# Mixers and branches with PE in program order, 32-column work gathered with one ada step at a time, denser background queues

## The chip, the cores and the metric

The kernel runs on one core of one Trainium2 chip. The metric is the device time of one execution in microseconds, as the median of several runs. TensorE is called PE, VectorE DVE, ScalarE ACT, GpSimd POOL and SyncE SP.

## What is computed

One layer of a hybrid decoder trunk, in float32, for a prompt of 256 tokens and for 8 samples that each take one step from a stored state. D_MODEL is 2048, a branch is 1024 wide.

```python
mod = jax.nn.silu(c) @ p['w_ada'][l] + p['b_ada'][l]          # six parts: shift, scale, gate, twice
sh1, sc1, gt1, sh2, sc2, gt2 = jnp.split(mod[:, None, :], 6, axis=-1)
h = rmsnorm(x, p['g_pre_mix'][l]) * (1.0 + sc1) + sh1
z = h @ p['w_in'][l]
(z_uv, hq, hf, hi, hg, gq, gk, gv, gr, glr, z_gate) = jnp.split(z, offsets, axis=-1)
...
y_a = spatial_gating(u, v, sgu_w_s, sgu_b_s)                  # A: causal 128x128 mixing per group
o_hg, S_hg = gated_linear_recurrence(q_hg, k_hg, hi, log_f, s_hg[l])   # B: HGRN2, 8 heads of 128 x 128
o_g, S_g = gated_linear_recurrence(q_g, k_g, gv, log_a, s_gla[l])      # C: GLA, 4 heads of 128 x 256
...
merged = gates[:, :, 0] * (branches[0] @ p['w_branch'][l, 0])
for n_b in range(1, N_BRANCH):
    merged = merged + gates[:, :, n_b] * (branches[n_b] @ p['w_branch'][l, n_b])
out = merged @ p['w_out'][l]
x = x + gt1 * rmsnorm(out, p['g_post_mix'][l])
h2 = rmsnorm(x, p['g_pre_mlp'][l]) * (1.0 + sc2) + sh2
y2 = jnp.square(jax.nn.relu(h2 @ p['w_mlp_up'][l])) @ p['w_mlp_down'][l]
x = x + gt2 * rmsnorm(y2, p['g_post_mlp'][l])
```

The recurrence is S_t = diag(f_t) S_{t-1} + k_t v_t^T with o_t = S_t^T q_t for each head; the kernel computes the prompt's by halving (differences over 1, 2, 4, ..., 128 positions), the samples' in one step. Outputs are y for prompt and samples, the final states, and the samples' normalised v rows.

## The kernel before

Activations lie feature by token: 128 features on the partitions, 264 columns (256 prompt tokens and 8 samples). Each weight matrix streams through once in blocks of 512 KB (class `Stream`): a block is loaded by SP three blocks ahead into one of six `raw` buffers and split two blocks ahead into a rounded part `whi` (L102, on ACT) and a remainder `wlo` (L99, on DVE). `granule` multiplies one block with the activations, split likewise: three products for each 128x128 tile (L459, L460, L461), 24 products for a block. A granule is the unit in which the text counts the program's progress. All granules of the program hold 13,872 products.

Other work is written as generators in three queues, which `linear` advances after each granule by the rates in `RATES` (background, samples, ada; another triple in each stage): `bg` holds the mixers, `bs` the samples' steps, `ba` the modulation. A generator runs up to its next `yield`, and the yield's number is what the step cost of the allowance.

- `ada_round` (L247): one part of the modulation. A step (L265) is four products of 32 output columns each, side by side in four strips of the PE array, over 512 streamed columns.
- `mixer_a` (L563): branch A. `mixer_r` (L813): the prompt's recurrence for a group of four heads, two HGRN2 groups and one GLA group. `small_level` (L852) computes a level of the halving in 32 products of 32 x 32; the levels of 32 (L908) and 64 (L916) positions use 32- and 64-column tiles. Then come the keys' transposes (L942), the final states (L950, L951), the outputs (L973 to L976) and their transposes (L995).
- `samples_r` (L762): the samples. Each of 32 steps takes one tile of states `st` (four HGRN2 heads or two GLA heads of one sample), loads the state two steps ahead (L777, three buffers), scales it on ACT (L791), adds the outer product on DVE (L793), stores it from POOL (L794), and reads it on PE with 32-column products (L799).
- `branch` (L1034): eight pairs of a gate product (`zin`) and a branch product with `w_branch`. `parts()`, which finishes the mixer and splits its output for the branch product, is called after the first gate product. `finish` (L1001) transposes the samples' outputs (L1008).

The framework's scheduler places the instructions on every engine, PE too; each engine then works off its list in order. PSUM tiles `sm` for all of the small work have three buffers, the products' accumulators `mm` two.

Of the kernel before, what the change touches and what calls it, by code (L numbers as in the profile page):

```python
# [35 lines left out]
RATES = ((1.7, 0.2, 0.3), (1.5, 0.35, 0.32), (1.5, 0.25, 0.28), (1.0, 0.05, 0.22))  # L36
ST_BUFS = 3
# [9 lines left out]
FILL = (5.0, 9.0)  # L47


@with_exitstack  # L50
def hybrid_step_kernel(
# [53 lines left out]
    # ---------------------------------------------------------------- constants  # L105
# [7 lines left out]
    # ---------------------------------------------------------------- small vectors  # L113
# [7 lines left out]
    # x: prompt rows as two token tiles, the samples' feature tiles as rows  # L121
# [53 lines left out]
    def sum_features(v, n, w):  # L175
        """Sums of v [P, n, w], which it overwrites, over its features (partitions and n tiles), on every partition."""
        while n > 1:
            n //= 2
            add(v[:, 0:n, :], v[:, 0:n, :], v[:, n:2 * n, :])
        ps = sm([P, w])  # L180
        T.matmul(ps, ones, v[:, 0, :], start=True, stop=True)
        return ps

    # ---------------------------------------------------------------- x normed and transposed
    def norm_rows(x, xs, xsn, r):
        """r [P, 2] = the prompt rows' 1 / rms; xsn = the samples' rows xs [P, KT, NS] over their rms."""
# [7 lines left out]
        ps = sum_features(sq, KT, NS)  # L194
# [5 lines left out]
    def transposed(x, k):  # L200
        """Columns of feature tiles k and k + 1 of the prompt rows, in PSUM [P, 2, NP]."""
# [29 lines left out]
    # ---------------------------------------------------------------- adaLN  # L231
# [6 lines left out]
    def ada_rows(acc, n):  # L238
        """PSUM rows (32 j + c, columns) -> [P, i, j, c] with the columns' features on the partitions."""
        am = tmp([P, 512], "am", 1)  # L240
        S.copy(am[:, 0:n], acc[:, 0:n])
        ps = sm()
# [4 lines left out]
    def ada_round(r, pre=()):  # L247
        """Part r of the modulation; pre are its first blocks of weights."""
# [12 lines left out]
        for k in range(KT):  # L261
            if k + 1 < KT:
                ws.append(load(2 * k + 2))
            for j in range(4):
                T.matmul(acc[32 * j:32 * j + 32, :], cT[:, k, :], ws[j // 2][:, j % 2 * 512:j % 2 * 512 + 512], start=k == 0, stop=k == KT - 1)  # L265
            del ws[0:2]
            if k + 1 < KT:
                ws.append(load(2 * k + 3))
# [1027 lines left out]
```

## Time and profile before

| | us |
|---|---|
| median of 3 runs (2008.63 to 2014.89) | 2010.1 |
| span of the profiled execution | 2009.9 |
| PE busy (matmul) | 1948.6, 97% |
| DVE busy | 1191.6, 59% |
| ACT busy | 1002.0, 50% |
| HBM read and written | 439.3 MB, 219 GB/s |

The span lies within 0.2 us of the median, so the profiled execution stands for the timed ones. Products are pipelined: the page's mean of 288 ns is the time from start to end of one product, while the next one starts after less than half of that. So the starts in a timeline tell how fast PE goes, not the durations. The page's chain of waits is on PE for 91% of the span.

### The profile page before, as it was taken

Reading aid. Unit: us, or ns where it says so; the run is one execution under the profiler, and the core shown is the slowest. Engines: PE = TensorE matmul, PEld = TensorE weight load, DVE = VectorE, ACT = ScalarE, POOL = GpSimd, SP = SyncE. Lnnn points to the kernel's source line nnn. Section 1 sums busy time; section 2 is a strip of 40 time slices with the busy share of each in tenths; the row PEclk is TensorE's granted clock in tenths of the full one; section 3 lists DMA queues with packets and bytes.
Section 4 is the critical chain, followed back from the end, with each engine's and each line's share of the span. In section 5 each row is a group of like instructions: output and inputs, shape, how many; then the busy total and the mean of one; then the engine's idle time right before and its main releaser. Section 6 shows DMA issues by size and latency. Waiting matters only on the chain.

```text
span 2009.9 us, 42161 instructions
## 1 busy us (share of the span) xinstructions
PE 1948.6 (97%) x17020; PEld 1814.9 (90%) x17020; DVE 1191.6 (59%) x2105; ACT 1002.0 (50%) x1773; POOL 40.5 (2%) x66
## 2 busy tenths in 40 slices
PE   5999999999999999899899999999999999999997
PEld 4779898989988987789899995999999999999996
DVE  3456566777475687445555556555555555555656
ACT  4434354576664574454444445555444445454543
POOL 1000000000000000000000000000000000000000
PEclk9999999999999999999999999999999999999998
DMA  9887978787798668887555866655555555555552
GB/s 311 289 300 244 292 229 250 219 276 222 255 286 280 211 207 255 271 273 228 189 179 180 271 200 231 212 185 179 180 183 182 181 179 184 179 183 180 180 179 84
DMA packets 378179, 442.05 MB, mean 220 GB/s; under 512 B 14914, under 2 KB 339136, under 8 KB 377984
## 3 DMA queue, kind: packets, MB, share of 16 engines
q1 hardware_dynamic: 372592, 424.27, 66.7%
q0 software_dynamic: 4496, 13.90, 1.9%
q8 instruction: 133, 2.18, 0.4%
q10 hardware_dynamic: 896, 1.19, 0.2%
q14 instruction: 62, 0.51, 0.1%
HBM read 427.60 MB, written 11.70 MB: 219 GB/s over the span
## 4 chain that ended last, share of the span: by engine, by line
PE 91%; DMA 4%; DVE 2%; ACT 2%; issue 1%; SPq 0%; ACTq 0%; DVEq 0%
PE mm L459 28%; PE mm L460 27%; PE mm L461 27%; PE ada L265 3%; DMA st<-in_state_gla_dram 2%; PE ada L236 2%; DMA raw<-in_w_ada_dram 1%; PE sm L540 1%; PE sm L799 1%; DVE wlo L99 1%; ACT whi L102 1%; DMA raw<-in_w_in_dram 1%; PE sm L852 1%; DMA st<-in_state_hgrn_dram 0%; DMA b<-in_g_post_mix_dram 0%
## 5 line engine op out<-in xcount | busy, mean ns | idle before, releaser
L459 PE MATMUL mm<-b,whi 128*128 128x264 f32 x4624 | 1332.1, 288 | 17.3 <-ACT b L102 8.0
L460 PE MATMUL mm<-b,whi 128*128 128x264 f32 x4624 | 1321.9, 286 | 1.5 <-DVE b L99 1.5
L461 PE MATMUL mm<-b,wlo 128*128 128x264 f32 x4624 | 1317.3, 285 | 3.2 <-DVE wlo L99 3.2
L99 DVE TENSOR_TENSOR wlo<-raw,whi 128x512 fp32r<-128x512 f32 x1156 | 790.6, 690 | 654.1 <-ACT whi L102 616.3
L102 ACT CAST whi<-raw 128x512 fp32r<-128x512 f32 x1156 | 709.1, 619 | 799.5 <-PE mm L460 720.8
L459 PEld LDWEIGHTS mm<-b,whi 128*128 128x128 f32 x4624 | 873.4, 189 | 78.6 <-issue 31.4
L461 PEld LDWEIGHTS mm<-b,wlo 128*128 128x128 f32 x4624 | 872.8, 189 | 13.4 <-issue 7.2
L460 PEld LDWEIGHTS mm<-b,whi 128*128 128x128 f32 x4624 | 873.4, 189 | 11.4 <-issue 8.8
L96 DVE TENSOR_TENSOR b<-b,mm 128x528 f32<-128x528 f32 x136 | 94.9, 698 | 17.8 <-PE mm L461 17.7
L265 PE MATMUL ada<-raw,cT 128*32 128x512 f32 x464 | 75.6, 616 | 3.0 <-DMA raw<-in_w_ada_dram 3.0
L791 ACT ACTIVATE st<-st,fs 128x128 f32<-128x128 f32 (+1 forms) x96 | 37.0, 430 | 69.9 <-DMA st<-in_state_gla_dram 46.3
L793 DVE SCALAR_TENSOR_TENSOR st<-vbc,b,st 128x128 f32<-128x128 f32 (+1 forms) x96 | 33.9, 390 | 62.1 <-ACT st L791 49.0
L236 PE MATMUL ada<-raw,cT 128*32 128x256 f32 (+1 forms) x640 | 43.9, 359 | 3.0 <-DMA raw<-in_w_ada_dram 3.0
L93 DVE TENSOR_TENSOR b<-b,b 128x512 f32<-128x512 f32 (+1 forms) x47 | 33.7, 739 | 2.0 <-ACT b L869 1.6
L794 POOL DMA_DIRECT2D out_dram<-st x32 | 23.5, 736 | 411.0 <-DVE st L793 381.8
L236 PEld LDWEIGHTS ada<-raw,cT 128*32 128x32 f32 x640 | 14.8, 113 | 13.5 <-DMA raw<-in_w_ada_dram 3.7
L265 PEld LDWEIGHTS ada<-raw,cT 128*32 128x32 f32 x464 | 12.2, 110 | 15.7 <-DMA raw<-in_w_ada_dram 6.6
L99 DVE TENSOR_TENSOR b<-gt,b 128x528 fp32r<-128x528 f32 x32 | 22.6, 708 | 3.2
L93 DVE TENSOR_TENSOR gt<-vt 128x528 f32<-128x528 f32 x32 | 22.4, 700 | 0.0
L99 DVE TENSOR_TENSOR b<-b 128x1024 f32<-128x1024 f32 (+1 forms) x21 | 22.3, 1064 | 0.1
L1202 ACT ACTIVATE b<-vt 128x528 fp32r<-128x528 f32 x32 | 20.7, 647 | 1.0
L1196 ACT ACTIVATE vt<-mm 128x528 f32<-128x528 f32 x32 | 19.4, 607 | 0.0
(284 smaller groups left out, 729.5 us busy)
## 6 DMA issues: line engine op xcount, KB each, us to landing
raw<-in_w_in_dram SPq DMA_DIRECT2D x242, 512.0 KB, 5.3
raw<-in_w_ada_dram SPq DMA_DIRECT2D x164, 512.0 KB, 5.2
raw<-in_w_mlp_up_dram SPq DMA_DIRECT2D x128, 512.0 KB, 3.8
raw<-in_w_mlp_down_dram SPq DMA_DIRECT2D x128, 512.0 KB, 3.6
raw<-in_w_branch_dram SPq DMA_DIRECT2D x48, 512.0 KB, 5.1
raw<-in_w_out_dram SPq DMA_DIRECT2D x32, 512.0 KB, 4.3
raw<-in_w_ada_dram SPq DMA_DIRECT2D x32, 256.0 KB, 5.6
vbc<-vs_d SPq DMA_DIRECT2D x32, 256.0 KB, 6.7
```

The source lines that it names most:

```text
L93: V.tensor_tensor(o, a, b, op=ALU.mult)
L96: V.tensor_tensor(o, a, b, op=ALU.add)
L99: V.tensor_tensor(o, a, b, op=ALU.subtract)
L102: S.copy(hi, src)
L236: T.matmul(acc[32 * j:32 * j + 32, 0:n], cT[:, k, :], w[:, n * j:n * j + n], start=k == 0, stop=k == KT - 1)
L265: T.matmul(acc[32 * j:32 * j + 32, :], cT[:, k, :], ws[j // 2][:, j % 2 * 512:j % 2 * 512 + 512], start=k == 0, stop=k == KT - 1)
L459: T.matmul(o, a, xh(k + j), start=first and j == 0, stop=False)
L460: T.matmul(o, a, xl(k + j), start=False, stop=False)
L461: T.matmul(o, b, xh(k + j), start=False, stop=last and j == n - 1)
L791: S.activation(st[:, i, :], st[:, i, :], AF.Copy, scale=fs[:, h0 + i, b:b + 1])
L793: V.scalar_tensor_tensor(st[:, i, :], v[:, i, :], k[:, h0 + i, NP + b:NP + b + 1], st[:, i, :], ALU.mult, ALU.add)
L794: nc.gpsimd.dma_start(G.s_out(b, h0, nh), st)
```

## The change

From the first mixer to the last branch PE keeps the order in which the program is written (`tc.manual_schedule` for PE); the other engines are scheduled as before. In that stretch:

- 32-column work is marked by `yield NARROW` and held until a slot opens. `background`, which takes the place of the three calls after each granule, opens a slot when an ada step is nearly due (`SLOT_LATE`) or something held has waited (`SLOT_WAIT` granules): then one held piece of `bg`, one of `bs` and one ada step are issued one after the other.
- `yield READY` holds the following PE work until at least one more granule has been issued.
- All rates of the queues go up, and `st` gets four buffers.
- A sample's four heads are read together, also those of GLA, which stand in two tiles.
- The levels of 32 and 64 use eight products with full 128-column weights each, and read less of the result.
- Samples' rows are transposed with a full 128 x 128 tile (`srow`, zeroed once) instead of 32 or 64 rows.
- `parts()` comes ahead of the first gate product.
- The four products for GLA's decays (`wup`) go between the granules of the following product. `ada_round` loads both of its next blocks after its step.

Comments and docstrings are gone as well, which the diff leaves out.

```diff
-RATES = ((1.7, 0.2, 0.3), (1.5, 0.35, 0.32), (1.5, 0.25, 0.28), (1.0, 0.05, 0.22))
-ST_BUFS = 3
+RATES = ((1.8, 0.35, 0.36), (1.7, 0.45, 0.36), (1.6, 0.4, 0.36), (1.0, 0.4, 0.36))
+ST_BUFS = 4
...
+NARROW, READY = object(), object()
+SLOT_LATE = 0.9
+SLOT_WAIT = 3
+HELD_OWED = 4.0
...
         for k in range(KT):
-            if k + 1 < KT:
-                ws.append(load(2 * k + 2))
             for j in range(4):
                 T.matmul(acc[32 * j:32 * j + 32, :], cT[:, k, :], ws[j // 2][:, j % 2 * 512:j % 2 * 512 + 512], start=k == 0, stop=k == KT - 1)
-            del ws[0:2]
-            if k + 1 < KT:
-                ws.append(load(2 * k + 3))
+            ws = [load(2 * k + 2), load(2 * k + 3)] if k + 1 < KT else []
             yield
...
+        def step(self):
+            self.held = None
+            try:
+                c = next(self.g[0])
+                if c is NARROW or c is READY:
+                    self.held, self.at = c, now[0]
+                else:
+                    self.owed -= 1.0 if c is None else c
+            except StopIteration:
+                self.g.pop(0)
+
+        def open(self, kind):
+            return self.g and self.held is kind and self.at < now[0]
+
         def pump(self, n=1.0):
             self.owed += n
-            while self.g and self.owed > 0.0:
...
+            while self.g and self.owed > 0.0 and (self.held is None or self.open(READY)):
+                self.step()
...
+            if self.held is not None:
+                self.owed = min(self.owed, HELD_OWED)
+
+        def slot(self):
+            if self.open(NARROW):
+                self.step()
...
+    def background():
+        now[0] += 1
+        bg.pump(rate[0])
+        bs.pump(rate[1])
+        ba.owed = min(ba.owed + rate[2], SLOT_LATE) if ba.g else 0.0
+        held = [q for q in (bg, bs) if q.open(NARROW)]
+        if ba.owed >= SLOT_LATE or held and (not ba.g or ba.owed >= 0.0 or now[0] - min(q.at for q in held) >= SLOT_WAIT):
+            bg.slot()
+            bs.slot()
+            if ba.owed >= 0.0 and ba.g:
+                ba.step()
...
             granule(w, k0, kc, c0, width, [acc], xh, xl, kb, kb == 0, kb + kc == nk)
-            bg.pump(rate[0])
-            bs.pump(rate[1])
-            ba.pump(rate[2])
+            background()
...
+    order = tc.manual_schedule(engines={mybir.EngineType.PE})
+    order.__enter__()
     gen_a = mixer_a()
...
             nc.gpsimd.dma_start(G.s_out(b, h0, nh), st)
+            sts.append(st)
             yield 0.5
+            if h0 + nh < 4:
+                continue
+            yield NARROW
             ps = sm([P, dv])
-            for i in range(nh):
-                h = h0 + i
-                T.matmul(ps[32 * h:32 * h + 32, :], qm[:, h, b, :], st[:, i, :], start=True, stop=True)
...
+            for h in range(4):
+                T.matmul(ps[32 * h:32 * h + 32, :], qm[:, h, b, :], sts[h // nh][:, h % nh, :], start=True, stop=True)
+            sts = []
...
             mul(es, es, v4(q, 2 * m)[:, :, :, m:2 * m])
             yield
+            yield NARROW
             ps = small_level(e, e)
...
+            yield READY
+            ps = sm([P, 8, 64])
+            for h in range(4):
+                for hf in range(2):
+                    b = e[:, h, P * hf:P * hf + P]
+                    rhs = b.rearrange("p (n j) -> p n j", j=2 * m)[:, :, m:2 * m]
+                    T.matmul(ps[:, 2 * h + hf, :].rearrange("p (n j) -> p n j", j=m), b, rhs, start=True, stop=True)
+            yield
             if m == 32:
-                ps = sm([P, 8, 32])
-                for h in range(4):
-                    for b in range(4):
-                        r_ = 64 * (b % 2)
-                        T.matmul(ps[r_:r_ + 32, 2 * h + b // 2, :], e[:, h, 64 * b:64 * b + 32], e[:, h, 64 * b + 32:64 * b + 64], start=True, stop=True)
-                yield
-                S.copy(att[0:32, :, 32:64], ps[0:32])
-                S.copy(att[64:96, :, 96:128], ps[64:96])
+                S.copy(att[0:32, :, 32:64], ps[0:32, :, 0:32])
+                S.copy(att[64:96, :, 96:128], ps[64:96, :, 32:64])
             else:
-                ps = sm([P, 8, 64])
-                for h in range(4):
-                    for hf in range(2):
-                        T.matmul(ps[0:64, 2 * h + hf, :], e[:, h, P * hf:P * hf + 64], e[:, h, P * hf + 64:P * hf + 128], start=True, stop=True)
-                yield
                 S.copy(att[0:64, :, 64:128], ps[0:64])
...
+        yield READY
         for h0 in range(0, 4, nh):
             so = blk([P, nh, dv])
...
         for m in range(8):
+            if m == 0:
+                yh, yl = parts()
             z = zin(9232 + n * D + m * CW)
             gt = tmp([P, 2, NT], "gt")
             S.activation(gt, z, AF.Tanh, scale=0.5)
-            if m == 0:
-                yh, yl = parts()
...
     branch(2, lambda: parts_c(gates_c))

+    order.__exit__(None, None, None)
```

What it does to the order shows first on PE, in the middle of the GLA group. In the names, `sm` is a small PSUM tile, `ada` the accumulator of the modulation, `st` a sample's states; L852 is a level of the recurrence, L799 the samples' reading, L265 an ada step. Before, with 24 products (left out) between one run and the next:

```order
L852 MATMUL sm_9856<-b_9762 32x32 x32
L799 MATMUL sm_9889<-st_9442,b_9325 32x256 x2
...
L265 MATMUL ada_8946<-raw_9773,cT 32x512 x2
L265 MATMUL ada_8946<-raw_9779,cT 32x512 x2
...
L799 MATMUL sm_9983<-st_9600,b_9325 32x256 x2
```

After, in one run (L903 is the level, L852 the samples' reading, L274 the ada step), with the products on both sides:

```order
L486 MATMUL mm_9837<-b_8936,wlo_9707 128x264
L903 MATMUL sm_9872<-b_9797 32x32 x32
L852 MATMUL sm_9905<-st_9489,b_9024 32x256 x2
L852 MATMUL sm_9905<-st_9498,b_9024 32x256 x2
L274 MATMUL ada_8742<-raw_9758,cT 32x512 x2
L274 MATMUL ada_8742<-raw_9760,cT 32x512 x2
L484 MATMUL mm_9837<-b_8940,whi_9786 128x264
```

Three runs have become one, and two tiles of states are read in it. The second place is the start of branch C on PE: before, the transposes of the samples' outputs (L1008) stand behind the last product of the gate (`mm_11955`) and ahead of the branch product, whose input `b_12122` is made from them.

```order
L461 MATMUL mm_11955<-b_2689,wlo_11985 128x264
L1008 MATMUL sm_12112<-cst,os_1593_9599 128x128
L1008 MATMUL sm_12115<-cst,os_1593_9599 128x128
L459 MATMUL mm_12134<-b_12122,whi_12014 128x264
L460 MATMUL mm_12134<-b_12123,whi_12014 128x264
```

After, they (L1062) stand ahead of the first gate product (`mm_11954`), which reads activations that have long been there:

```order
L486 MATMUL mm_11793<-b_2689,wlo_11823 128x264
L1062 MATMUL sm_11932<-cst,os_1537_9229 128x128
L1062 MATMUL sm_11935<-cst,os_1537_9229 128x128
L484 MATMUL mm_11954<-b_330,whi_11852 128x264
L485 MATMUL mm_11954<-b_331,whi_11852 128x264
```

The transposes have moved up by the 96 products of one gate product. The third place is the same one on DVE: the copies out of the transposes (L1063), the scaling (L1140) and the split (L103 on `b`) that make the branch's input now alternate with splits of weights (L103 on `wlo`).

```order
L1063 COPY b_10899<-sm_11935 128x4x8
L1140 SCALAR_TENSOR_TENSOR b_10898<-b_10898,vec,b_11374 128x264 x2
L1140 SCALAR_TENSOR_TENSOR b_10898<-b_10898,vec,b_11375 128x264
L103 TENSOR_TENSOR wlo_11921<-raw_11894,whi_11920 128x512
L103 TENSOR_TENSOR wlo_11925<-raw_11894,whi_11924 128x512
L1140 SCALAR_TENSOR_TENSOR b_10898<-b_10898,vec,b_11375 128x264
L1140 SCALAR_TENSOR_TENSOR b_10899<-b_10899,vec,b_11374 128x264 x2
L1140 SCALAR_TENSOR_TENSOR b_10899<-b_10899,vec,b_11375 128x264
L103 TENSOR_TENSOR b_11943<-b_10898,b_11942 128x1056
```

Before, the same scaling (L1086 there) stood in one piece, with one split of weights ahead of it and the splits of the next two blocks behind it.

More of the change, by code (lines that the diff above doesn't have):

```diff
@@ L609, in mixer_a @@
         mul(w8, vs, vs)
-        ps = sum_features(w8, 8, NS)
-        yield 0.4
+        fold(w8, 8)
+        yield 0.3
+        yield READY
+        ps = sum_partitions(w8, NS)
+        yield 0.1
         rstd_small(ps, 1.0 / BW, r8)
@@ L931, in mixer_r @@
         yield
+        yield READY
         attx = blk([P, 4, P])
@@ L944, in mixer_r @@
             yield
+        yield READY
         for h0 in range(0, 4, nh):
@@ L988, in mixer_r @@
             yield
+        yield READY
         o = [blk() for _ in range(nj)]
```

88 lines of the change are left out of this document (45 added, 43 removed).

## The prediction

> **What bounds the kernel now.** First the page: the span, the engines' shares, and the costliest group.
>
> ```profile
> span 2009.9 us, 42161 instructions
> ...
> PE 1948.6 (97%) x17020; PEld 1814.9 (90%) x17020; DVE 1191.6 (59%) x2105; ACT 1002.0 (50%) x1773; POOL 40.5 (2%) x66
> ...
> L459 PE MATMUL mm<-b,whi 128*128 128x264 f32 x4624 | 1332.1, 288 | 17.3 <-ACT b L102 8.0
> ```
>
> PE is busy for 97% of the span; VectorE (DVE) and ScalarE (ACT) have room. The product lines L459, L460 and L461 run 4624 times each, 13,872 products of 264 columns, and the change leaves them all. The stage that it touches is that of the mixers and branches, which the busy time by windows shows:
>
> ```profile
> 332.00:970.00 638.00, 623.35 (x6101) 558.31 (x6100) 411.12 (x786) 359.42 (x710) 29.87 (x43) 0.99 0.78 247
> ```
>
> The columns are PE, PEld, DVE, ACT and POOL busy, the granted clock, the DMA share and GB/s. PE lacks 15 us of 638 here, so this stage is PE's as well. What can be won is PE time that is no product of the 13,872, and the waits. For the first I read the timeline of PE alone: how far a foreign piece of work pushes the products apart.
>
> ```profile
> 750.43 0.28 PE L461 MATMUL mm<-b,wlo 128*128 128x264 f32 x1
> 750.64 0.76 PE L852 MATMUL sm<-b 128*32 128x32 f32 x64
> ...
> 751.56 0.28 PE L460 MATMUL mm<-b,whi 128*128 128x264 f32 x1
> ...
> 757.16 0.28 PE L461 MATMUL mm<-b,wlo 128*128 128x264 f32 x1
> 757.37 1.06 PE L265 MATMUL ada<-raw,cT 128*32 128x512 f32 x8
> ...
> 758.59 0.29 PE L460 MATMUL mm<-b,whi 128*128 128x264 f32 x1
> ```
>
> From 751.56 to 757.16 stand 46 products: 5.60 / 46 = 0.1217 us each. From the last product before a foreign run to the second one after it, two products would take 0.243. One level of the recurrence (L852) takes 1.13, so it costs 0.89 us; one ada step (L265) takes 1.43 and costs 1.19. Both in one run:
>
> ```profile
> 629.26 0.28 PE L461 MATMUL mm<-b,wlo 128*128 128x264 f32 x1
> 629.47 0.73 PE L852 MATMUL sm<-b 128*32 128x32 f32 x62
> ...
> 630.05 1.04 PE L265 MATMUL ada<-raw,cT 128*32 128x512 f32 x6
> 631.25 0.28 PE L460 MATMUL mm<-b,whi 128*128 128x264 f32 x1
> ```
>
> 1.99 - 0.243 = 1.75 us, against 0.89 + 1.19 = 2.08 apart. So 0.33 us belongs to the passage from 128-column work to 32-column work and back, and is paid once for each visit. That is the price that the change goes for.
>
> **The change part by part.** *Visits.* Counted in the two built orders, from the first mixer transposes to the last branch product, PE goes to 32- or 64-column work and back 86 times before and 48 times after. 38 x 0.33 = **-12.5 us**. The ada steps are the same in number over the whole program.
>
> *Samples.* A GLA sample was served in two visits of two heads; now in one of four.
>
> ```profile
> 945.65 0.28 PE L461 MATMUL mm<-b,wlo 128*128 128x264 f32 x1
> 945.86 0.63 PE L799 MATMUL sm<-st,b 128*32 128x256 f32 x4
> ...
> 946.64 0.28 PE L460 MATMUL mm<-b,whi 128*128 128x264 f32 x1
> ```
>
> 0.99 - 0.243 = 0.75, of which 0.33 is the passage and 0.42 the work. The four row strips of an ada step overlap (0.86 us for four products of 512 columns, by the 1.19 above), so I let four heads cost what two did: 16 x 0.42 becomes 8 x 0.42, **-3.4 us**.
>
> *Levels of 32 and 64.* They leave narrow tiles for full 128-row, 128-column ones, eight products to a level.
>
> ```profile
> 486.19 0.28 PE L461 MATMUL mm<-b,wlo 128*128 128x264 f32 x1
> ...
> 487.26 0.28 PE L460 MATMUL mm<-b,whi 128*128 128x264 f32 x1
> ...
> 668.84 0.28 PE L461 MATMUL mm<-b,wlo 128*128 128x264 f32 x1
> ...
> 670.35 0.28 PE L460 MATMUL mm<-b,whi 128*128 128x264 f32 x1
> ...
> 680.61 0.29 PE L461 MATMUL mm<-b,wlo 128*128 128x264 f32 x1
> 680.74 1.06 PE L935 MATMUL sm<-b,b 128*128 128x128 f32 x8
> ...
> 681.75 0.28 PE L460 MATMUL mm<-b,whi 128*128 128x264 f32 x1
> ```
>
> Between the first two stands a level of 32 (L908): 0.83 us; between the next two a level of 64 (L916): 1.27. Without their passages, which are counted already, that is 0.50 + 0.94 = 1.44 a group, 4.3 for three groups. The new product is not in the trace. The nearest row is L935, with the same full weights but 128 columns streamed instead of 64: 0.90 for four, 0.225 each. If the streamed columns set it, it is half, 0.11. 48 of them cost 5.3 to 10.8; I take the upper end, as the weights are those of L935: **+6.5 us** (lower end +1.0).
> The Trainium skill, page "TensorE: Matmul & The Clock Gate", section "LDWEIGHTS (loading the stationary operand)", lets a load last its columns / 1.2 ns, whatever is streamed: it speaks against this edit. By it (an estimate) a 128-column load is 107 ns, two for a float32 product 0.213, 48 of them 10.2, which gives +5.9; by the streamed columns the edit would be nearly free. No run so far shows which.
>
> PE work together: -12.5 - 3.4 + 6.5 = **-9.4 us**; at the lower end of the new levels -14.9.
>
> *Parts ahead of the gate product.* Branch C starts like this now:
>
> ```profile
> 970.51 0.28 PE L461 MATMUL mm<-b,wlo 128*128 128x264 f32 x1
> ...
> 973.80 1.07 ACT L102 CAST b<-b 128x1056 fp32r<-128x1056 f32 x1 [1.96 <-DVE b L1086]
> ...
> 974.93 0.49 PE L459 MATMUL mm<-b,whi 128*128 128x264 f32 x1 [3.91 <-ACT b L102]
> ...
> 981.98 0.28 PE L461 MATMUL mm<-b,wlo 128*128 128x264 f32 x1
> ```
>
> The gate product ends at 970.51, and the branch's input is made only then: 18 product intervals and two transposes, about 2.4 us, take 11.47. **-9.1 us**. After, the transposes stand ahead of the gate's 96 products (96 x 0.1217 = 11.7 us), and in the built DVE order the scaling stands among the weight splits of that product, two casts of 1.07 beside it. The cover exceeds the 9.1 by 2.6; without it all 9.1 come back. Branches A and B start the same way; I count nothing for them.
>
> *Waits for the states.* What PE and ACT waited for from 335 to 985, when the states land, and three windows:
>
> ```profile
> PE mm L459 <- ACT whi L102: 7.9, 4, 3.6
> PE sm L950 <- ACT b L943: 3.7, 1, 3.7
> ...
> ACT st L791 <- DMA st<-in_state_gla_dram: 46.3, 12, 7.9
> ACT st L791 <- DMA st<-in_state_hgrn_dram: 21.0, 7, 6.2
> ...
> DMA to landing us min/median/max: 2.6/5.7/9.5
> ...
> 650.80:657.60 6.80, 5.12 (x22) 4.89 (x23) 4.54 (x9) 4.85 (x11) 1.06 (x2) 0.50 0.59 192
> 790.70:794.10 3.40, 3.40 (x76) 3.10 (x75) 2.37 (x6) 1.50 (x3) 0.45 (x1) 0.51 0.98 306
> 852.20:859.00 6.80, 5.97 (x20) 3.05 (x20) 4.65 (x8) 3.14 (x7) 1.03 (x2) 0.50 0.69 229
> ```
>
> ACT stands in order: a state that hasn't landed holds up the casts of weights behind it, and then PE (7.9 + 3.7 = 11.6 us). After such waits the clock was at half for 17.0 us, 8.5 lost. So 20.1 us hang on this. A fourth buffer moves a state's release further ahead of its use (for HGRN in the built ACT orders 2.6 granules of weight splits on the mean before, 3.2 after), and a GLA sample now waits once for its pair instead of twice; READY puts a granule between the keys' transposes and the final states (the 3.7). But GLA's first state of a pair still stands two granules behind its release, some 6 us, where 5.7 is the median landing. I take half: **-10 us**, bounds 0 and -20.
>
> *Fixed order and denser queues.* What is new is that PE can't step around an input that is late; behind it wait the next products, and so everything. Nearly each reader stands a granule (24 x 0.1217 = 2.9 us) behind its writer. At two places four tiles of transposes follow each other on three PSUM buffers, at most a 3.7 like that of L950 each. DVE and ACT: if the mixers' last PE work comes at product 5,208 instead of 5,808 of a stage from 1,944 on, the time shrinks to 0.84; even if all of DVE's 411 and ACT's 359 of 638 us went into that, it is 77% and 67%. Bounds 0 and +15; I take **+4**.
>
> Sum against the profiled execution: 2009.9 - 9.4 - 9.1 - 10 + 4 = **1985.4 us**. Its span is 0.2 below the median of 2010.1, so no shift is made: 1985.
>
> **The rivals.** *The waits only move* (0.25). For it: ACT's 67 us of waiting come from landings, which no edit shortens, and the work gets denser. Then -9.4 - 9.1 stand, the -10 doesn't come, and +8 is new: 1999, between 1995 and 2010.
> *The gathering saves no more than it costs* (0.08). If 0.33 holds for two pieces but a visit of three is held up by the latest of them, or full-width levels cost more than L935: the -9.4 becomes 0 and the rest stays, 1995. Against it: the order shows the gathering done as told, nearly each level and sample stands in a run with an ada step.
> *Slower* (0.09). One mechanism: in each of GLA's samples 3 to 8 the pair of states lands after PE has reached its reading. PE now stands still in its order, and as at 650, where 3.6 us of waiting were followed by 6.8 at half clock, each costs 3.6 + 3.4 = 7.0: 6 x 7.0 = 42, and the -10 is not had. 2009.9 - 18.5 + 42 = 2033. It decides if a landing takes more than the two granules to ACT's place and the two to three from there to PE's, some 12 us; 9.5 is the longest seen.
> *The short waits and the clock* (inside the +4). Before the window at 790.7 stands this wait:
>
> ```profile
> PE mm L459 <- ACT whi L102: 2.4, 1, 2.4
> ```
>
> 2.4 us of waiting were followed by 3.4 at half clock, 4.1 together, so a new wait of that size would count 1.7 more. The Trainium skill, page "TensorE: Matmul & The Clock Gate", Part 1, halves the clock only after an idle window of some 3.4 us; by it a wait of 2.4 adds nothing more, and the +4 would be +2 to +3. The row disagrees and decides.
> *Better* (0.08): levels at their lower price and all 20 us of waits gone: 2009.9 - 14.9 - 9.1 - 20 = 1966.
>
> **How the numbers follow.** Forecast 0.50 (1977 to 1995), the others as given. A measurement of this kernel can tell 0.3%, 6 us, from no change: 2004 to 2016. Of the first rival 0.10 lies there, so faster is 0.50 + 0.15 + 0.08 + 0.08 = 0.81, same 0.10, slower 0.09. The range leaves out the better and the slower case: 1972 to 2008.
>
> **What would show it.** Right: 32-column runs of about 1.75 us with two kinds in them; branch C's first product within 1 us of the gate's last; ACT waiting clearly less than 67 us for states; fewer than four half-clock windows in this stage; the full-width levels at 1.8 us. Wrong: waits of PE over 15 us in this stage on lines that didn't wait before, or casts of weights behind states of GLA with PE behind them.

## The result and the profile after

The change makes the kernel slower: 2032.1 us (median of 4 runs, 2028.9 to 2036.3) beside 2009.4 for the kernel before on the same chip (2007.9 to 2014.9). The ratio is 1.0104, with an interval of 1.0083 to 1.0126. Forecast was 1985.

First the page of the kernel after, with its span, its engines and its costliest group (busy time and mean of one, then the idle time before it and who ended it):

```profile
span 2027.1 us, 42047 instructions
...
PE 1951.1 (96%) x16972; PEld 1824.0 (90%) x16972; DVE 1185.5 (58%) x2097; ACT 1001.0 (49%) x1773; POOL 40.7 (2%) x67
...
L484 PE MATMUL mm<-b,whi 128*128 128x264 f32 x4624 | 1332.0, 288 | 14.6 <-ACT whi L106 10.9
```

PE's share has fallen from 97 to 96% over a longer span: it isn't busier, it waits more. The busy time by windows, for the stretch shown of before (PE, PEld, DVE, ACT, POOL, clock, DMA share, GB/s):

```profile
332.00:970.00 638.00, 600.13 (x5820) 540.67 (x5819) 389.68 (x755) 345.21 (x685) 29.88 (x43) 0.97 0.77 238
```

PE was busy for 623 of these 638 us, now for 600, at a mean clock of 0.97 instead of 0.99. So the loss sits in the stage that the change touches. Who waits there, from the view of waits (in total, times, longest; PE from 330 to 1000, ACT and DVE from 335 to 985):

```profile
PE mm L486 <- DVE wlo L103: 12.9, 13, 5.2
PE mm L484 <- ACT whi L106: 10.9, 4, 7.1
PE ada L274 <- DMA raw<-in_w_ada_dram: 6.1, 5, 2.5
PE sm L1004 <- ACT b L1007: 4.1, 1, 4.1
PE sm L852 <- ACT b L989: 2.2, 1, 2.2
...
ACT st L841 <- DMA st<-in_state_gla_dram: 52.5, 9, 8.9
ACT st L841 <- DMA st<-in_state_hgrn_dram: 31.7, 7, 8.0
...
DVE st L843 <- DMA vbc<-vs_d: 26.5, 8, 6.1
```

PE waits for split weights. The engines that split them wait for samples: ACT 84 us for states (67 before), DVE 26.5 us for the broadcast value rows `vbc`. Before, DVE has no such row; 13.2 us of waiting at the same instruction are put down there to two weight loads, which it doesn't read, so some of that may have been value rows too. How the one becomes the other, in the timeline of ACT, PE and SP around the longest wait (start, duration, instruction, idle time before it):

```profile
759.33 0.69 ACT L922 ACTIVATE b<-b 128x512 f32<-128x512 f32 x1
767.89 0.91 ACT L841 ACTIVATE st<-st,fs 128x256 f32<-128x256 f32 x2 [7.88 <-DMA st<-in_state_gla_dram]
768.71 1.12 ACT L106 CAST whi<-raw 128x512 fp32r<-128x512 f32 x2
...
762.00 0.28 PE L486 MATMUL mm<-b,wlo 128*128 128x264 f32 x1
769.36 0.59 PE L484 MATMUL mm<-b,whi 128*128 128x264 f32 x1 [7.08 <-ACT whi L106]
...
757.78 0.42 SPq L826 DMA_DIRECT2D st<-in_state_gla_dram  x1
762.91 8.12 SPq L444 DMA_DIRECT2D raw<-in_w_in_dram  x2
```

The state asked for at 757.78 is there only when ACT goes on at 767.89, 10 us later. Behind it in ACT's order stands the cast of the next weights, and behind that PE's next product: 7.08 us of standing still. SP is held up too, since its next block of weights waits for a buffer that isn't split yet. Then comes the clock; the three longest windows at half clock are:

```profile
581.20:588.00 6.80, 6.11 (x90) 5.87 (x94) 6.47 (x12) 1.70 (x4) 0.75 (x1) 0.50 0.80 222
...
765.50:775.70 10.20, 6.34 (x60) 5.88 (x64) 7.24 (x14) 6.47 (x14) 1.08 (x2) 0.50 0.74 240
...
857.70:864.50 6.80, 5.62 (x20) 5.08 (x21) 3.42 (x6) 2.87 (x7) 2.56 (x4) 0.50 0.87 288
```

With three more of 3.4 us each there are six windows, 34.0 us at half clock (three and 17.0 us before, up to the start of branch C).

**An account of the stage.** For each kernel I take the time from the start of product 1944 to that of product 7068 in the trace: 5124 x 0.1215 = 622.6 us for the products, then the foreign work priced as in the prediction (0.33 for each visit, and the clean price of each piece), and a rest, which is waits and half clock. So the foreign work is a count at the prediction's prices; it is not measured a second time:

```
                stage   foreign work (visits)   rest
before          787.5   130.8 (87)              34.1, of it 7.9 at branch C's start
after           807.7   121.0 (48)              64.1, of it 0.0 there
```

By this count the foreign work fell by 9.8 us, branch C's start by 7.9, and the other waits rose from 26.2 to 64.1, by 37.9. The sum is +20.2; the span grew by 17.2, the other 3 us were won outside the stage. (Between just these two products the trace has 86 visits before, one fewer than the count used here; that would move 0.3 us from the foreign work to the rest.)

### The profile page after: what moved, and what is told of

The parts are those of the page before. It is cut to its first block, busy times and chain, and to the rows that moved or that the text cites. A ratio compares the mean times of both kernels' runs of the same rounds, so it can differ in the third digit from the quotient of the medians.

```text
span 2027.1 us, 42047 instructions
## 1 busy us (share of the span) xinstructions
PE 1951.1 (96%) x16972; PEld 1824.0 (90%) x16972; DVE 1185.5 (58%) x2097; ACT 1001.0 (49%) x1773; POOL 40.7 (2%) x67
## 3 DMA queue, kind: packets, MB, share of 16 engines
q1 hardware_dynamic: 372592, 424.27, 68.0%
q8 instruction: 133, 2.18, 0.5%
## 4 chain that ended last, share of the span: by engine, by line
PE 86%; DMA 8%; issue 3%; DVE 2%; ACT 1%; SPq 0%; POOL 0%; DVEq 0%; ACTq 0%; POOLq 0%
PE mm L484 26%; PE mm L485 26%; PE mm L486 25%; PE ada L274 3%; DMA raw<-in_w_ada_dram 2%; DMA st<-in_state_gla_dram 2%; PE ada L244 2%; DMA vbc<-vs_d 1%; DMA st<-in_state_hgrn_dram 1%; PE sm L576 1%; DVE wlo L103 1%; PE sm L214 1%; ACT whi L106 0%; PE sm L963 0%; DMA out_dram<-st 0%
## 5 line engine op out<-in xcount | busy, mean ns | idle before, releaser
L484 PE MATMUL mm<-b,whi 128*128 128x264 f32 x4624 | 1332.0, 288 | 14.6 <-ACT whi L106 10.9
L103 DVE TENSOR_TENSOR wlo<-raw,whi 128x512 fp32r<-128x512 f32 x1156 | 790.2, 690 | 662.7 <-ACT whi L106 630.8
L274 PE MATMUL ada<-raw,cT 128*32 128x512 f32 x464 | 77.6, 615 | 9.1 <-DMA raw<-in_w_ada_dram 6.1
L841 ACT ACTIVATE st<-st,fs 128x128 f32<-128x128 f32 (+1 forms) x96 | 36.1, 428 | 84.2 <-DMA st<-in_state_gla_dram 52.5
L274 PEld LDWEIGHTS ada<-raw,cT 128*32 128x32 f32 x464 | 13.9, 110 | 23.7 <-DMA raw<-in_w_ada_dram 15.8
L244 PEld LDWEIGHTS ada<-raw,cT 128*32 128x32 f32 x640 | 14.9, 113 | 13.5 <-DMA raw<-in_w_ada_dram 4.1
L103 DVE TENSOR_TENSOR b<-gt,b 128x528 fp32r<-128x528 f32 x32 | 22.7, 708 | 3.3
L103 DVE TENSOR_TENSOR b<-b 128x1024 f32<-128x1024 f32 (+1 forms) x21 | 22.3, 1066 | 0.0
```

The costliest lines, as they stand in the source:

```text
L103: V.tensor_tensor(o, a, b, op=ALU.subtract)
L244: T.matmul(acc[32 * j:32 * j + 32, 0:n], cT[:, k, :], w[:, n * j:n * j + n], start=k == 0, stop=k == KT - 1)
L484: T.matmul(o, a, xh(k + j), start=first and j == 0, stop=False)
L841: S.activation(st[:, i, :], st[:, i, :], AF.Copy, scale=fs[:, h0 + i, b:b + 1])
```

## The experiments

Every run was compared with the kernel before on its own chip. The chips differ: the medians of the kernel before run from 2007.4 to 2011.9. So what a run wins beside the change is taken below from the ratios, where 0.0010 is 2.0 us and the change's loss is 21 us; an interval reaches 2 to 5 us to either side. Rest and visits are counted as above, from one profiled execution each, which lies up to 5 us from the run's median; where an expectation says 65, 36 or 26 us of waits, it is the same count made a little differently (64, 35 and 24 here).

| run | median us | ratio to before, 95% | foreign | rest |
|---|---|---|---|---|
| the change | 2032.1 | 1.0104 (1.0083 to 1.0126) | 121.0 | 64.1 |
| e1 parts alone | 2001.6 | 0.9957 (0.9941 to 0.9974) | 130.4 | 24.2 |
| e2 old rates of samples | 2019.9 | 1.0055 (1.0035 to 1.0076) | 121.4 | 51.3 |
| e3 old rates of ada | 2023.6 | 1.0070 (1.0050 to 1.0090) | 121.7 | 57.8 |
| e4 all old rates | 2018.9 | 1.0045 (1.0030 to 1.0060) | 121.0 | 53.2 |
| e5 ada loads as before | 2027.0 | 1.0086 (1.0065 to 1.0106) | 121.0 | 61.6 |
| e6 states three ahead | 2027.3 | 1.0083 (1.0062 to 1.0105) | 121.0 | 59.7 |
| e7 half samples | 2023.1 | 1.0067 (1.0044 to 1.0090) | 125.7 | 55.2 |
| e8 before, new rates | 2037.1 | 1.0132 (1.0109 to 1.0154) | 126.1 | 66.7 |
| e9 spread | 2014.7 | 1.0040 (1.0025 to 1.0055) | 122.0 | 48.2 |
| e10 table only | 2012.7 | 1.0024 (1.0013 to 1.0035) | 121.7 | 41.5 |
| e11 fewer bytes | 1975.1 | 0.9846 (0.9829 to 0.9862) | 121.0 | 8.0 |
| e12 no fixed order | 2029.2 | 1.0114 (1.0098 to 1.0129) | 121.0 | 61.5 |
| e13 no state stores | 2023.0 | 1.0060 (1.0040 to 1.0079) | 121.0 | 58.5 |
| e14 value rows once | 1981.2 | 0.9852 (0.9831 to 0.9874) | 121.0 | 10.6 |
| e15 third value buffer | 2023.0 | 1.0059 (1.0036 to 1.0082) | 121.0 | 57.7 |
| e16 parts, fewer bytes | 1984.9 | 0.9873 (0.9855 to 0.9891) | 130.4 | 3.5 |
| e17 rows side by side | 2001.9 | 0.9957 (0.9942 to 0.9973) | 121.0 | 34.8 |
| e18 rows and table | 1990.8 | 0.9905 (0.9881 to 0.9928) | 121.7 | 21.1 |

**One part alone, and the old rates in the change.** e1 moves only `parts()` in the kernel before; e2 to e4 put columns of the old table back into the change.

```diff
 # e1, in branch() of the kernel before
+            if m == 0:
+                yh, yl = parts()
             z = zin(9232 + n * D + m * CW)
 # e4; e2 and e3 take over the second or the third column alone
-RATES = ((1.8, 0.35, 0.36), (1.7, 0.45, 0.36), (1.6, 0.4, 0.36), (1.0, 0.4, 0.36))
+RATES = ((1.7, 0.2, 0.3), (1.5, 0.35, 0.32), (1.5, 0.25, 0.28), (1.0, 0.05, 0.22))
```

> The kernel before with one edit: parts() ahead of the first gate product of each branch. Every theory of the slowdown agrees here: the 9.1 us at branch C's start go, 2001 us (1999 to 2004). If it stays within 3 us of the kernel before, the wait at branch C's start came back elsewhere and the trace of the change misled.

> The change with the samples' rates of before (0.2, 0.35, 0.25, 0.05), all else as changed. Theory 1, the samples' states and value rows land too late for the denser queue, and ACT and DVE stand in order before them with the weights' splits behind: most of the 35 us of new waits go, 2000 us (1995 to 2010), ACT waits for states under 70 us and DVE for value rows under 15. Theory 2, the denser ada queue: 2028 to 2034. Theory 3, holding the 32-column work: 2028 to 2034.

> The change with the ada rates of before (0.3, 0.32, 0.28, 0.22), all else as changed. Theory 2, ada weights come late or crowd the queue of SP and the raw buffers: 2000 to 2012, PE's waits for ada weights in the stage gone. Theory 1: 2024 to 2032, the waits for states stay at 80 us. Theory 3: 2028 to 2034.

> The change with all rates of before (background, samples, ada). Theories 1 and 2: 1990 to 2002, as the PE work is 9.8 us shorter and branch C's start 8 us. Theory 3, the held work and the fixed order make the waits whatever the rates: over 2015.

e1 came out as forecast: -8.1 us beside the kernel before in the same series (2009.7). The old rates bring back 10, 7 and 12 us of 21, so density has a part in the loss but seems to be less than all of it. e4 came out where the theory of held work and fixed order had it, over 2015. In e4 the old rate of the mixers leaves a group unfinished at a branch's start; by the account 11.9 us of its rest lie in one run of those leftovers at 702 us. So going back isn't the same as taking density away. But without the leftovers e4's rest is still 41.3 us, against 24.2 in e1, which has the same rates and only `parts()` of the change, although ACT waits less for states in e4 (62 us, against 75). So the changed kernel has some 17 us of waits that its rates don't explain, and no run here isolates their cause. What follows is the opposite test, and with it the change's other parts.

**Density alone, and the parts around the loads.** e8 gives the kernel before the new table and nothing else. e5, e6 and e7 take back or loosen one part of the change, e12 the fixed order.

```diff
 # e5, in ada_round
+            if k + 1 < KT:
+                ws.append(load(2 * k + 2))
             for j in range(4):
                 T.matmul(acc[32 * j:32 * j + 32, :], cT[:, k, :], ws[j // 2][:, j % 2 * 512:j % 2 * 512 + 512], start=k == 0, stop=k == KT - 1)
-            ws = [load(2 * k + 2), load(2 * k + 3)] if k + 1 < KT else []
+            del ws[0:2]
+            if k + 1 < KT:
+                ws.append(load(2 * k + 3))
 # e6, in samples_r (states and value rows are then fetched by two functions; the first lines of that are left out)
-            if n + 2 < len(steps):
-                fetch(*steps[n + 2])
+            if n + 3 < len(steps):
+                fetch_st(*steps[n + 3])
+            if n + 2 < len(steps):
+                fetch(*steps[n + 2])
 # e7, in samples_r (the lines that collect the halves, and the sum of the results by halves, are left out)
-            for h in range(4):
-                T.matmul(ps[32 * h:32 * h + 32, :], qm[:, h, b, :], sts[h // nh][:, h % nh, :], start=True, stop=True)
+            for i in range(nh):
+                h = h0 + i
+                T.matmul(ps[32 * h:32 * h + 32, :], qm[:, h, b, :], st[:, i, :], start=True, stop=True)
 # e12
-    order = tc.manual_schedule(engines={mybir.EngineType.PE})
-    order.__enter__()
```

> The changed kernel, but an ada step asks for its next weights as before: one block ahead of its products and one behind them (after the change both are asked for only behind them). Theory 'ada loads': the runs with L274 came late because their weights did (PE 6.1 and PEld 11.9 us of waits on raw<-in_w_ada in the stage of the mixers and branches); this run loses about 12 us of 2032, to 2020, and those two rows fall below 3 and 5. Theory 'states' (the loss is ACT standing for states of samples, with the casts of weights behind it): the time stays within 2028 to 2035 and ACT's waits for states stay near 84 us.

> The changed kernel, but a sample's state is asked for three steps ahead instead of two (its four buffers allow it; the broadcast value rows stay two ahead). Theory 'states': ACT's 84 us of waits for states fall below 45, PE's waits for whi (10.9) and for L1007's output (4.1) go with them and so do half-clock windows: about 2012 to 2018. Theory 'ada loads' or 'density': ACT's waits fall, the time does not, 2028 to 2035. If the landing itself gets later because more is asked for at once, ACT's waits stay near 80.

> The changed kernel, but each half of a GLA sample is read by PE in a visit of its own, as before the change, so its state buffer comes free without waiting for the other half. PE's own work grows by 8 x 0.42 = 3.4 us and by 4 visits (52 for 48 in the built order) x 0.33 = 1.3. Theory 'pairs hold the buffers': ACT's waits for GLA states fall from 52 us below 30 and the time is 2032 + 4.7 - 15 to 20, about 2017 to 2022. Theory 'density' (the pair is not the cause, the rates are): the waits stay and it is about 2037.

> The kernel before with nothing but the new table of rates: its queues as dense as in the change, nothing gathered, three state buffers, transposes behind the gate product. Its built order has 74 visits to 32- and 64-column work instead of 87: 13 x 0.33 = -4.3 us. Theory 'density costs by itself': ACT's and DVE's waits for states and PE's waits behind them grow as in the change, +13 us (what going back to the old rates won in the change), to about 2018. Theory 'density costs only with gathering': 2005.

> The changed kernel without the fixed PE order: the scheduler places PE's instructions. The built PE order differs in 12 lines only. Theory 'density': nothing changes, 2028 to 2036. Theory 'the fixed order makes PE stand where it could step around': below 2022.

e8 decides that density alone is enough: the new table makes the kernel before 28 us slower (27 by the ratio), at least as much as the whole change, with no pairs, slots or fixed order in it; about 2018 was the most that was expected. Its foreign work fell by 4.7, its rest rose from 34.1 to 66.7, and ACT waited 81 us for states, which landed in 6.5 us at the median (5.7 before). PE's three largest waits in e8 have the sources of the change's:

```profile
PE mm L459 <- ACT whi L102: 13.6, 7, 4.8
PE mm L461 <- DVE wlo L99: 6.9, 12, 1.4
PE ada L265 <- DMA raw<-in_w_ada_dram: 6.2, 5, 3.3
```

None of the others explains much: e5 and e6 win 4 us and e12 none, all within the intervals; e7 wins 7, with intervals that just overlap and ACT's waits for GLA states unchanged (52.8 us), so it is not the pair that holds them up. Asking earlier hardly helped either: in e6 ACT still waited 46.4 us for GLA states. As neither the time of asking nor the time of reading did much, the next thing to try is how long a transfer takes.

**The transfers.** A sample's step moves 256 KB of state in, 256 KB out, and 256 KB of value rows, which is 2 KB read by 128 partitions. e11 leaves out the stores and loads value rows for two steps of a group only; e13 and e14 do one of the two; e15 leaves nothing out and moves a buffer from the states to the value rows; e16 is e11's edit on e1's kernel.

```diff
 # e13 (and e11, e16)
-            nc.gpsimd.dma_start(G.s_out(b, h0, nh), st)
 # e14 (and e11, e16)
-            v = tmp([P, 4, P], "vbc", VB_BUFS)
-            nc.sync.dma_start(v, vs_d[G.i, h * nj:h * nj + 4, b, :].partition_broadcast(P))
+            if len(vbs) < 2:
+                v = tmp([P, 4, P], "vbc", VB_BUFS)
+                nc.sync.dma_start(v, vs_d[G.i, h * nj:h * nj + 4, b, :].partition_broadcast(P))
+                vbs.append(v)
+            v = vbs[h // nh % 2]
 # e15
-ST_BUFS = 4
-VB_BUFS = 2
+ST_BUFS = 3
+VB_BUFS = 3
```

> The changed kernel at its own dense rates, but with fewer bytes for each step of a sample: the state is loaded and computed, while the samples' states are not stored and the broadcast value rows are loaded for two steps of a group only and used again (a step moves 256 KB instead of 768; the stored states, and the samples' results with them, are left out or other). Built PE order as in the change. Theory 'transfers' (density costs because weights, ada weights, states and value rows together ask for more than the transfers deliver, so each lands later): ACT's waits for states fall below 50 and PE's waits with them, 2032 - 20 or more, below 2012. Theory 'buffers' (a state's buffer comes free too late): leaving the store out frees it earlier too, but a whole step of lead was worth only 5 us, so not below 2024.

> The changed kernel with only the stores of the samples' states left out (32 of 256 KB; that output is left out). Theory 'bytes': stores and value rows have the same bytes, so this run gets about half of the 57 us, about 2003. Theory 'value rows' (DVE stands 26.5 us for them, ahead of the weight splits whose buffers the next loads wait for): little, above 2018. Theory 'stores' (they are in the way of the loads): nearly all, below 1988.

> The changed kernel with only the value rows loaded for two steps of a group and used again (26 of 32 loads of 256 KB left out; the samples' results are others). Theory 'bytes': about half of the 57 us, about 2003. Theory 'value rows': nearly all, below 1988. Theory 'stores': above 2018.

> The changed kernel with three buffers for states and three for value rows (four and two in the change), nothing left out, same PE order. Theory 'bytes': nothing but landings move, 2025 to 2036. Theory 'value rows, by their two buffers' (the load of the next rows goes out only when DVE is done with the one before): DVE's 26.5 us of waits for them go, and the time falls by 10 or more, below 2022.

> The kernel before with the parts ahead of the gate product (2001.6 before), and with the states not stored and the value rows used again, as in the run of the change that took 1975. Its waits of 26 us in the stage should fall to about 9 as there: 2001.6 - 17 = 1985. Then the gathering alone is worth 1985 - 1975 = 10, near the forecast 9.4. If it falls to 1975 too, the gathering wins nothing even without waits; if it stays above 1995, the transfers hurt the gathered kernel only.

Without these transfers the dense change takes 1975.1 us, and its rest is 8.0. Nearly all of its 52 us is the value rows: 51 us without them, 9 without the stores, although these are 32 of the same size and the value rows left out only 26 (but the stores go outward, from another queue), and 9 with a third buffer, which was taken from the states. So the number of bytes alone doesn't explain it, and a want of buffers hardly. The waits in e14, for which the change's 12.9, 10.9, 6.1, 52.5 and 31.7 stand above:

```profile
PE mm L486 <- DVE wlo L103: 1.6, 5, 0.7
PE mm L484 <- ACT whi L106: 1.3, 2, 0.8
PE ada L274 <- DMA raw<-in_w_ada_dram: 0.8, 2, 0.5
...
ACT st L844 <- DMA st<-in_state_hgrn_dram: 19.3, 7, 4.6
ACT st L844 <- DMA st<-in_state_gla_dram: 17.6, 7, 3.5
```

The value rows delayed the others' transfers, not only their own reader: without them ACT's waits for states fall from 84 to 37 us, and the states land in 5.2 us at the median, where the change has 6.7 (least, median, most, from 335 to 985 us):

```profile
DMA to landing us min/median/max: 2.7/5.2/8.6
```

The six loads of value rows that e14 keeps still take 7.2 us at the median and 6.0 at the least, where the change's 32 had 7.2 and 5.6; so it isn't their number that makes them slow.

e16 against e11 asks what gathering is worth when hardly anything waits. The count says 130.4 - 121.0 = 9.4 us of foreign work. The stage itself is 4.9 us shorter (756.5 to 751.6), as the rest is 3.5 in e16 and 8.0 in e11. By the ratios it is 5.4 us, with intervals that overlap. So in these two executions the gathering wins, but only about half of what the count says; the gathered kernel keeps a few more waits.

**Sparser, and the rows side by side.** e9 and e10 spread the queues in the change. e17 lays a sample's value rows side by side in DRAM, so that each partition reads one piece of 2 KB and not four of 512 B; e18 is e17 with e10's table.

```diff
 # e9 also: self.owed = min(self.owed, 0.0 if self is bs else HELD_OWED)
+RATES = ((1.8, 0.3, 0.25), (1.7, 0.35, 0.25), (1.6, 0.3, 0.25), (1.0, 0.3, 0.25))
 # e10, e18
+RATES = ((1.8, 0.25, 0.3), (1.7, 0.35, 0.3), (1.6, 0.3, 0.3), (1.0, 0.3, 0.3))
 # e17, e18; sample_rows writes its columns sample by sample to match
-    vs_d = dp.tile([3, 8, NS, P], F32, tag="vs_d", name="vs_d")
+    vs_d = dp.tile([3, 8 * NS, P], F32, tag="vs_d", name="vs_d")
-            nc.sync.dma_start(v, vs_d[G.i, h * nj:h * nj + 4, b, :].partition_broadcast(P))
+            r0 = (4 * b + h) * nj
+            nc.sync.dma_start(v.rearrange("p k v -> p (k v)"),
+                vs_d[G.i, r0:r0 + 4, :].rearrange("k v -> (k v)").partition_broadcast(P))
```

> The changed kernel with its queues spread out again: rates of the samples 0.3, 0.35, 0.3, 0.3 and of the ada steps 0.25 throughout (the mixers' own rates stay as the change has them), and the samples' queue keeps no backlog while it stands at a held visit, so that the two halves of a GLA sample don't follow each other at once. Built order: 51 visits (48 in the change), the last state read at product 5808 (5040 in the change, 5808 before). Theory 'density' (its 30 us of new waits come from asking for weights of ada steps and states faster than they land): the stage's waits fall from 65 us to about 30, 2032 - 35 + 1 = 1998. Theory 'the gathering itself holds things up' (pairs, slots, full blocks asked for behind the step): no better than the run with the old rates, 2012 to 2020.

> The changed kernel with nothing but a table between the two: samples 0.25, 0.35, 0.3, 0.3, ada steps 0.3 throughout, the mixers' rates as in the change. 50 visits, the last state read at product 5232. Theory 'density': most of the 35 us come back, 2003 to 2010. Theory 'gathering': 2015 to 2020, as with each of the two old columns alone (2020 and 2024).

> The changed kernel at its own rates, nothing left out: the value rows of a sample lie side by side in DRAM, so that each partition reads one piece of 2 KB instead of four of 512 B. Theory 'pieces': the value rows land in about half the time (3.5 to 4.5 us instead of 7.2), and the time falls to between 1980 and 1995. Theory 'same source' (128 readers of the same 2 KB) or 'bytes': they land as late as before and the time stays within 2022 to 2036.

> The changed kernel with the value rows side by side and the sparser table (samples 0.25, 0.35, 0.3, 0.3, ada steps 0.3), nothing left out. If the two were independent: 2032 - 30 - 19 = 1983. If both cure the same queue of transfers, the waits of the stage go from 36 us to about 20, 1988 to 1993. If the rest has another cause, 1998 to 2004.

e10 wins 16 us with a table alone. e9, whose samples are spread further and keep no backlog, wins 13: they end so late that the branches wait for their outputs, as its largest wait of PE says:

```profile
PE sm L1062 <- ACT os L862: 11.3, 2, 6.4
```

The two intervals overlap, so which density is better isn't shown. Neither run came to what 'density' had forecast (1998, and 2003 to 2010), and e9 lies where 'the gathering itself' had it, though 11.3 us of its waits are for the late outputs. e17 wins 30 us at the full density, with nothing left out. The same bytes go in 12,288 packets fewer (360,304, of 372,592), three fewer for each partition and load. The landings from 335 to 985 us, from the views of single tiles (least, median, most): the states and the value rows in the change, then the value rows in e17:

```profile
DMA to landing us min/median/max: 2.8/6.7/12.6
```

```profile
DMA to landing us min/median/max: 5.6/7.2/12.3
```

```profile
DMA to landing us min/median/max: 3.3/5.3/8.4
```

The expectation for small pieces (3.5 to 4.5 us, 1980 to 1995) was too good: the layout is worth 30 of the 51 us. Whether the rest comes from 128 readers of one source, from the bytes, or from the rows' place in SP's queue was not tried. e18 lies in the range of "one cause" (1988 to 1993) at 1990.8 us: each edit helps less when the other is there. In the account e17 takes 29.3 us off the change's rest and e10 22.6, and both together 43.0. The ratios alone can't tell this from independence, which would be 0.9877 and lies only just outside e18's interval. It is the fastest complete version here, 0.9905 (0.9881 to 0.9928) of the kernel before, with 50 visits where the change has 48.

## Why the prediction was wrong

- **PE's work** (-9.4): -9.8 by the count, with 87 visits before and 48 after. Its prices held where nothing waited. In the change, a run of a level, four GLA heads and an ada step stands between these two products:

```profile
753.97 0.28 PE L486 MATMUL mm<-b,wlo 128*128 128x264 f32 x1
...
756.39 0.28 PE L485 MATMUL mm<-b,whi 128*128 128x264 f32 x1
```

  756.39 - 753.97 - 0.243 = 2.18 us, and one passage with the three pieces at the prediction's prices is 0.33 + 0.56 + 0.42 + 0.86 = 2.17. So three pieces pay one passage, and four heads cost what two did. The levels of full width, from the same timeline:

```profile
490.85 0.28 PE L486 MATMUL mm<-b,wlo 128*128 128x264 f32 x1
490.97 1.89 PE L963 MATMUL sm<-b 128*128 128x64 f32 x16
492.67 0.37 PE L484 MATMUL mm<-b,whi 128*128 128x264 f32 x1
492.88 0.28 PE L485 MATMUL mm<-b,whi 128*128 128x264 f32 x1
```

  492.88 - 490.85 - 0.243 = 1.79 us for eight products, 0.223 each, as with twice the columns: the upper end, as taken, so the streamed columns don't set it. By the Trainium skill, page "TensorE: Matmul & The Clock Gate", section "LDWEIGHTS (loading the stationary operand)", a load lasts its columns / 1.2 ns, whatever is streamed; two loads of 128 columns make 0.213, an estimate, and this run's 0.223 is within 5% of it.
- **Parts ahead of the gate product** (-9.1): shown. e1 alone measured -8.1, and in the change branch C's first product starts 0.12 us after the gate's last.
- **Waits for the states** (-10) and **fixed order and denser queues** (+4): here it failed. Together -6 was forecast on 26.2 us of waits, and they rose by 37.9. The step at fault is the +4: it asked whether DVE (77%) and ACT (67%) could do the work in 0.84 of the time, and not whether the transfers could bring it. The table of rates alone costs 28 us on the kernel before (e8), nearly twice the +15 that was the term's upper bound. In the change, 51 us hang on the loads of value rows (e14) and 30 of them on those rows' layout (e17). Some 17 us that are left at the old rates (e4 against e1) have no cause shown. The -10 then rested on a median landing of 5.7 us, which was that of the sparser queues. By the view of the transfers the GLA states land in 8.2 us in the change (5.8 before):

```profile
st<-in_state_gla_dram SPq DMA_DIRECT2D x16, 256.0 KB, 8.2
```

  The same view of the kernel before had the sign. For the same 256 KB, and by the code the same 512 B pieces as HGRN's states, the value rows took half as long again:

```profile
vbc<-vs_d SPq DMA_DIRECT2D x32, 256.0 KB, 6.7
...
st<-in_state_hgrn_dram SPq DMA_DIRECT2D x16, 256.0 KB, 4.5
```

- **The fixed order** itself: nothing (e12), neither the harm feared nor a gain.
- **The rival "slower"** named 2033, and 2032 came, but not by its mechanism. PE's one wait listed at a reading of states (L852, 2.2 us) is put down to ACT's copy of another product's result (L989); the others are mainly for weights split late, for ada weights and for ACT's scaling of the final states (L1007). Reading each half alone (e7) won 7 us at most, and e8 loses 28 with no pairs at all. "The gathering saves no more than it costs" is not borne out where hardly anything waits (4.9 us won in the stage, e16 against e11), and with the waits it stays open. "The waits only move" had the right place (ACT's waits come from landings, and none of the change's edits shortens one), but priced it at +8.
- Of what was to be seen, the full-width levels and branch C came; ACT's waits rose instead of falling, and there were six half-clock windows, not fewer than four. Of the signs of being wrong, casts of weights stood behind states of GLA with PE behind them, as at 759 to 769 us.

## What to carry to other kernels

A denser background queue is first a denser queue of transfers: count what it asks for in its densest stretch, and read how long each kind of transfer takes to land, before the busy shares of the engines. Where one kind lands later than another of the same size, mend its layout ahead of any schedule: here one changed layout won 30 us. Whether the gathering then pays is not shown by that: e17 comes to the same ratio as e1 (0.9957), which has the old layout and only `parts()` of the change, and e1 with the new layout was not run. A part of a change that seems harmless (a table of rates) is tested by itself on the old kernel, since taking it back in the new one mixes its effect with that of the rest.

## What the chip showed that was not expected

Loads of 256 KB in which all partitions read the same 2 KB in four pieces never landed in under 5.6 us in the change, against 2.8 for a state of that size; in one piece they took 3.3 at the least. And the DMA's busy share didn't tell whether PE was fed. From 730 to 890 us, where PE waits most, the windows show for the change, then for the rows side by side (e17), then for e11:

```profile
730.00:890.00 160.00, 137.54 (x1364) 118.22 (x1363) 88.72 (x172) 71.45 (x147) 12.86 (x18) 0.93 0.81 254
```

```profile
730.00:890.00 160.00, 151.04 (x1472) 133.87 (x1472) 93.07 (x179) 83.95 (x172) 12.88 (x18) 0.97 0.87 275
```

```profile
730.00:890.00 160.00, 159.93 (x1543) 145.26 (x1542) 97.14 (x183) 89.49 (x178) 2.03 (x3) 1.00 0.80 249
```

At a share of 0.81 and 254 GB/s PE lacked 22 us of 160; with another layout the same program moved 275 GB/s and PE had 13.5 us more of work in the same time. Without most of the value rows and the stores PE lacked nothing, at a share of 0.80 and 249 GB/s. How long the states took to land told the three apart (6.7, 5.7 and 4.7 us at the median), and the share did not.
